# A decoder block on one core: the last LayerNorm split between two phases, new constants in the kernel's clock, and short products traced with a lag

## The chip, the core and the metric

The kernel runs on one NeuronCore of a Trainium2 chip. The metric is the device time of one execution in microseconds (us), the median of several runs. The engines are TensorE (PE: matmuls, with the weight loads as PEld), VectorE (DVE), ScalarE (ACT), GpSimd (POOL) and SyncE (SP), which issues all DMAs. Each engine takes its instructions strictly in the order of its own queue; an instruction waits on semaphores for results of other engines and for DMAs. So the order in each queue, fixed when the program is built, decides who waits for whom.

## The reference

One block with two causal token mixers beside each other, on 2048 tokens of width 1024:

```python
h = _rmsnorm(x, norm_g) * (1 + scale) + shift
p = h @ w_in                       # 9344 columns, split into the parts below
u = val * sigmoid(gate);  u = causal_depthwise_conv(u, width 31)
u = _layernorm(u);  y_conv = (silu(u) * silu(og)) @ w_conv_out
r, k, v, w_low, a_low = token_shift(ts, mu)
o = rwkv7_scan(r, decay, k, v, kk, kk * a)      # 16 heads of 64, a delta-rule state
o = groupnorm(o) + sum(r * k * r_k) * v
y_rwkv = (o * silu(r_og)) @ w_rwkv_out
m = sigmoid(g_conv) * y_conv + sigmoid(g_rwkv) * y_rwkv
x = _rmsnorm(x + gate * (m @ w_out)) * final_g
```

## The kernel before

Tokens are worked on in 4 blocks of 512, features on partitions, 8 tiles of 128 x 512 for 1024 features. Each float32 product is three passes: the weights and the activations are split into a high and a low part (w_hi, w_lo, h_hi, h_lo), and h_hi with w_hi, h_lo with w_hi and h_hi with w_lo are summed, so a projection of one output tile is 8 x 3 = 24 matmuls of 512 columns into a PSUM tile ps_main.

**First phase.** Per block there are 73 projections with w_in. A block has four slots (function `slot`), one for each group of four heads (two pairs). A slot projects k, r and v of both pairs (`proj`, with the token shift in `shifted`), and between them the conv tiles ("c", function `conv`, whose 31 taps are `taps`, VectorE operations on a PSUM tile acc) and the gates ("1" to "4"); `order` and the tables `FILL` and `LAST` set the sequence. The function `pair` makes the operands of the scan out of k, r and v with short products into the PSUM tile aux: lw and la (decay and learning rate), sq (norms of k), KR with BK (two times eight products, masked by VectorE into As), transposes of BK into tk, rh (the bonus term rk) and a transpose of vv. The function `group` then inverts the triangular blocks (POOL's loop over itmp and TT, with detours over DRAM: dA, dT) and runs the chain: 8 chunks, each with a few products into xo, a VectorE addition to uv and four VectorE updates of the state S. After the chain the group norm follows, a transpose (late<-ident,uv), and the result goes to z in DRAM.

Beside these, `side_work` does the next block's RMSNorm, the LayerNorm of the conv branch for the block before (`lnorm_first`: sum of the eight y tiles, mean by a product with ones, squares, variance, rsqrt, then per tile mult, tanh, scale, mult, mult), and splits weights of later products ahead (`presplit`). The LayerNorm of the last block is a task of its own (`last_norm`), which starts when the last convolution is done. Its result u goes to u in DRAM. The phase ends with the output projections of block 0 (`rows0`, "ro" and "co"), which run while the last group's chain ends.

**Order by a clock.** The first phase is not scheduled by the compiler: the program is traced once in Python, and a clock of its own (`note`) counts for every engine when it would be free, with constants for each kind of operation (`RATE`, line 56; a DMA issue counts 0.36 us). `now` is TensorE's time. Every helper is a generator that yields a condition such as `ok(tile)` (ready by the clock); `poll` lets all tasks go on whose condition is met, after each k step (three matmuls) of a projection. A short product outside the chain yields `burst(...)`: it goes at once when its operands are ready, except that during a chain, when no other product has been traced since the last k step, it waits up to `JOIN` = 2.0 us for one:

```python
            if r is None or r > now[0] or joined[0] or not chains[0]:
                return r
            return r + JOIN
```

A slot begins with `until(lambda: not Gs[:-1] or Gs[-2].normed)`: it lets the clock run until the group two before is normalized, whose buffers it takes.

**Second phase.** For each block: the products with w_out into pout (four column parts cb), the residual added into xt, the final RMSNorm and the store of xt; in between the next block's products with w_rwkv_out (`rproj`) and w_conv_out (`cproj`), whose inputs are loaded from z and u in DRAM and split (`lsplit`). Here the order comes from the tile framework's own scheduler. The ring of loads has 8 buffers (`LDB`). The eight xt tiles of a block share their buffers with the eight mr tiles (result of `rproj`) of the next.

In the profile nearly every instruction has line 132, the helper that records it; groups are told apart by their tiles.

Of the kernel before, what the change touches and what calls it, by code (L numbers as in the profile page):

```python
# [45 lines left out]
SLACK = 2.0  # L46
KEPT = ("in",)
# [4 lines left out]
FIRST = 5  # L52
AHEAD = 0.7
BANKS = {"aux": 2, "late": 1, "xo": 2}
SEM, JOIN = 0.1, 2.0
# [19 lines left out]
def hybrid_block(ctx: ExitStack, tc: tile.TileContext, x, vecs, convk, w2a2, final_g, ada, w_in, w_co, w_ro, w_o, crow, out,  # L75
                 seq=2048, groups=(0, 1, 2, 3), phase2=True, dbg=None):
    NB = seq // TB
    now, tasks, kind, joined, chains = [0.0], [], [None], [False], [0]
# [3 lines left out]
    def size(ap):  # L82
        return math.prod(ap.shape[1:])
# [192 lines left out]
    u_dram = scratch("u_d")  # L276

# [245 lines left out]
    hx = Ring(HXB, hx0)  # L523
    t2r = Ring(T2B, lambda name: e2.tile([P, TB], F32, name=name, tag="t2", bufs=T2B))
# [252 lines left out]
    def pair(G, q_, box):  # L777
        b, pr, uv, Asb = G.b, 2 * G.g + q_, G.uv, G.As[q_]
# [37 lines left out]
        yield ok(k)  # L816
        KR = l3.tile([P, NCH // 2, 4 * CH], F32, name="KR", tag="KR", bufs=KRB)
# [75 lines left out]
        yield when(lambda: "v" in box)  # L893
# [14 lines left out]
    def opened(b, g, h, lora):  # L908
        G = Group()
        G.b, G.g, G.h, G.lora, G.tri, G.pairs, G.chained, G.gated, G.normed = b, g, h, lora, 0, 0, False, False, False  # L910
        G.uv = l3.tile([P, NCH, 2, P], F32, name="uv", tag="uv", bufs=2)
        G.dN = dp.tile([2, 2, NCH // 2, 2, 2, 32], F32, name="dN", tag="dN", bufs=3)
        G.As = [l3.tile([P, 2, NCH, P], F32, name="As", tag="As", bufs=ASB) for _ in range(2)]
        G.R = [{}, {}]
        return G
# [4 lines left out]
    def group(G, before):  # L920
        g, b, As, uv, R = G.g, G.b, G.As, G.uv, G.R
# [51 lines left out]
        yield when(lambda: G.pairs == 2 and (before is None or before.chained))  # L973
        yield ok(*As)
# [79 lines left out]
        locked[0] = False  # L1054
# [135 lines left out]
    convs = []  # L1190

    def taps(b, j, u, before):
# [18 lines left out]
    def lnorm_first(b, hx):  # L1211
# [9 lines left out]
        yield hx.room(3, 1)  # L1221
        ys, nxt = yload(0), yload(1)
        for j in range(1, KT):
            yj = nxt
            if j + 1 < KT:
                yield hx.room(1, 1)
                nxt = yload(j + 1)
            yield ok(ys, yj)
            eng.tensor_tensor(out=ys, in0=ys, in1=yj, op=ALU.add)
            hx.give(yj)  # L1230
# [34 lines left out]
        hx.give(qs, rt, mean)  # L1265
        def both_of(j):
            yj, ct = yload(j), hx.take("lnc")
            nc.sync.dma_start(ct, co_dram[b][j])
            return yj, ct

        nxt = None
        for j in range(KT):
            if nxt is None:
                yield hx.room(3, 1)
                nxt = both_of(j)
            else:
                yield hx.room(1)
            yj, ct = nxt
            th, nxt = hx.take("lnth"), None
            if j + 1 < KT and b + 1 == NB and hx.room(2)() is not None:  # L1280
                nxt = both_of(j + 1)
# [80 lines left out]
    def sides(b, g):  # L1362
# [6 lines left out]
        if b and g == (0 if b + 1 == NB else 1):  # L1369
            yield from lnorm_first(b - 1, hx)  # L1370
            if b + 1 == NB:
                yield from lend(3)
# [24 lines left out]
    def last_norm():  # L1397
        yield when(lambda: len(convs) == KT * NB and convs[-1].done)
        yield from lnorm_first(NB - 1, more)
# [14 lines left out]
    def order(b, g):  # L1414
# [11 lines left out]
        for q in range(2):  # L1426
            for name, t_ in (("k", T_K), ("r", T_R), ("vv", T_V)):
                yield name, q, t_ + 2 * g + q
            yield from fill(FIRST if q == 0 else len(todo))
# [16 lines left out]
    def slot(b, g, h, lora, new):  # L1446
        until(lambda: not Gs[:-1] or Gs[-2].normed)
        G = opened(b, g, h, lora)
        reached[0] += 1
        groups_.append(Task(group(G, Gs[-1] if Gs else None), 0))  # L1450
        Gs.append(G)
        items, box, hfs = list(order(b, g)), {}, []
        for n, it in enumerate(items):
            rest = len(items) - n
            if new is not None and rest == 4:
# [121 lines left out]

    def cproj(b, uhl, mhl):
# [41 lines left out]
    for b in range(NB):  # L1620
# [73 lines left out]
        if b + 1 < NB:  # L1694
            uhl = lsplit(u_dram[b + 1], utiles())
# [40 lines left out]
```

## Time and profile before

| | us |
|---|---|
| median of 3 runs (2885.52 to 2889.45) | 2889.28 |
| the profiled execution | 2893.26 |
| its span, first to last instruction | 2891.5 |
| TensorE busy | 2722.4 |
| VectorE busy | 2067.5 |
| GpSimd busy | 1195.6 |
| ScalarE busy | 1092.9 |
| mean granted TensorE clock | 0.984 |

A row of groups reads: line, engine, operation, out<-in tiles, shapes and count, then busy us and mean ns of one, then the engine's idle time just before them and what ended it. A row of waits reads: who waited, for whom, us in total, number of waits, the longest. A row of stretches reads: the stretch and its length, then busy us (and instructions) of PE, PEld, DVE, ACT and POOL, the granted TensorE clock, the DMA share and GB/s.

### The profile page before, as it was taken

The page shows a single profiled execution, that of the slowest core. Times are in us where ns is not written, and L with a number is a line of the kernel's source. Part 1 is how long each engine was busy: PE and PEld are TensorE (multiplying, and loading weights), DVE is VectorE, ACT ScalarE, POOL GpSimd, SP SyncE. Part 2 cuts the span into 40 slices and gives each one's busy share as a digit, 9 for nine tenths or more (in the row PEclk, how much of TensorE's full clock was granted, in tenths as well). Part 3 has the DMA queues.
Part 4 walks back from the last instruction along what each step waited for, and adds up shares of the span by engine and source line. Part 5 has one row for each costly group of instructions (what it writes and reads, how often), then busy time and mean ns, then how long its engine had stood idle before and what let it go on. Part 6 is the DMA issues. An engine that isn't in the chain of part 4 may idle for free. (4 is left out here: it accounts for less than half of the span.)

```text
span 2891.5 us, 52406 instructions
## 1 busy us (share of the span) xinstructions
PE 2722.4 (94%) x19472; PEld 2195.2 (76%) x19472; DVE 2067.5 (72%) x3598; ACT 1092.9 (38%) x2181; POOL 1195.6 (41%) x1725
## 2 busy tenths in 40 slices
PE   6999999989999999999999998999999998999998
PEld 5777777767777777777777776877777777898988
DVE  6877887869677878886878786888887576343343
ACT  5545444434243434443434343324343334121211
POOL 1564746533528364534564553474543612000000
PEclk9999999989999999999999999999999999999999
DMA  8776867666758677767666776676665778777664
GB/s 329 258 286 206 292 218 265 236 233 228 235 185 290 199 255 242 275 222 238 231 251 223 249 255 197 220 269 215 227 230 191 273 247 315 259 239 247 215 226 175
DMA packets 370959, 697.26 MB, mean 241 GB/s; under 512 B 135184, under 2 KB 153936, under 8 KB 370704
## 3 DMA queue, kind: packets, MB, share of 16 engines
q1 hardware_dynamic: 370704, 693.91, 70.3%
q8 instruction: 154, 2.52, 0.4%
q14 instruction: 101, 0.83, 0.1%
HBM read 500.63 MB, written 192.02 MB: 240 GB/s over the span
## 5 line engine op out<-in xcount | busy, mean ns | idle before, releaser
L132 PE MATMUL ps_main<-h_hi,w_hi 128*128 128x512 f32 x2432 | 1016.3, 418 | 16.7 <-DVE lora L132 4.6
L132 PE MATMUL ps_main<-h_hi,w_lo 128*128 128x512 f32 x2432 | 966.9, 398 | 25.3 <-POOL w_lo L132 14.6
L132 PE MATMUL ps_main<-h_lo,w_hi 128*128 128x512 f32 x2432 | 961.3, 395 | 0.5 <-DVE h_lo L132 0.5
L132 DVE SCALAR_TENSOR_TENSOR acc<-u,ck,acc 128x512 f32<-128x512 f32 x928 | 698.0, 752 | 27.9 <-POOL u L132 2.2
L132 PEld LDWEIGHTS ps_main<-h_hi,w_lo 128*128 128x128 f32 x2432 | 462.2, 190 | 140.1 <-POOL w_lo L132 18.7
L132 PEld LDWEIGHTS ps_main<-h_hi,w_hi 128*128 128x128 f32 x2432 | 463.3, 190 | 128.4 <-issue 13.3
L132 PEld LDWEIGHTS ps_main<-h_lo,w_hi 128*128 128x128 f32 x2432 | 463.7, 191 | 96.3 <-issue 8.7
L132 POOL TENSOR_TENSOR w_lo<-w_st,w_hi 128x1024 fp32r<-128x1024 f32 (+1 forms) x82 | 165.0, 2012 | 332.5 <-ACT w_hi L132 288.5
L132 ACT ACTIVATE th<-ps_main 128x512 f32<-128x512 f32 x160 | 95.5, 597 | 360.2 <-PE ps_main L132 311.5
L132 POOL TENSOR_TENSOR TT<-TT,itmp 128x126 f32<-128x126 f32 (+22 forms) x496 | 209.5, 422 | 38.9
L132 POOL TENSOR_TENSOR itmp<-La,TT 128x126 f32<-128x126 f32 (+22 forms) x496 | 203.5, 410 | 37.7 <-issue 7.9
L132 ACT CAST w_hi<-w_st 128x1024 fp32r<-128x1024 f32 (+1 forms) x135 | 127.4, 945 | 221.6 <-DMA w_st<-w_co_t 78.4
L132 DVE SCALAR_TENSOR_TENSOR S<-xo,pe,Se 64x64 f32<-64x64 f32 x512 | 145.0, 283 | 91.9 <-PE xo L132 69.4
L132 ACT COPY uv<-xo 64x256 f32<-64x256 f32 (+1 forms) x192 | 81.2, 439 | 251.3 <-PE xo L132 184.7
L132 DVE TENSOR_TENSOR w_lo<-w_st,w_hi 128x1024 fp32r<-128x1024 f32 x53 | 74.5, 1405 | 68.3 <-PE ps_main L132 51.6
L132 DVE TENSOR_TENSOR As<-aux,maskA 128x512 f32<-128x512 f32 x128 | 82.3, 685 | 49.0 <-PE aux L132 48.9
L132 ACT ACTIVATE Se<-S,pe 128x128 f32<-128x128 f32 x256 | 89.0, 397 | 67.2 <-DVE S L132 66.7
L132 PEld LDWEIGHTS aux<-KR,BK 64*128 64x128 f32 x1024 | 66.3, 191 | 44.3 <-POOL KR L132 21.1
L132 PE MATMUL aux<-KR,BK 64*128 64x128 f32 x1024 | 80.0, 290 | 20.7 <-POOL KR L132 14.0
L132 POOL TENSOR_TENSOR wlo<-wf,wl 64x128 fp32r<-64x128 f32 x64 | 31.3, 489 | 159.2 <-ACT wl L132 156.7
L132 DVE TENSOR_TENSOR xt<-pout,xt 128x256 f32<-128x256 f32 x64 | 24.4, 420 | 100.1 <-PE pout L132 100.1
L132 PEld LDWEIGHTS xo<-S,KR 128*128 128x128 f32 x512 | 77.1, 189 | 20.7 <-ACT Se L132 4.3
(283 smaller groups left out, 5005.4 us busy)
## 6 DMA issues: line engine op xcount, KB each, us to landing
w_hi<-kh_in SPq DMA_DIRECT2D x219, 512.0 KB
w_lo<-kl_in SPq DMA_DIRECT2D x219, 512.0 KB
w_st<-w_in_t SPq DMA_DIRECT2D x73, 512.0 KB
kh_in<-w_hi SPq DMA_DIRECT2D x71, 512.0 KB
kl_in<-w_lo SPq DMA_DIRECT2D x71, 512.0 KB
lny<-y_d SPq DMA_DIRECT2D x96, 256.0 KB
w_hi<-kh_ro SPq DMA_DIRECT2D x32, 512.0 KB
w_lo<-kl_ro SPq DMA_DIRECT2D x32, 512.0 KB
```

The costliest lines, as they stand in the source:

```text
L132: r = f(*a, **k)
```

## The change

Six things are changed.

1. **The lag.** `burst` adds `lag[0]` = `LAG` = 1.0 us to the time at which its operands are ready; with `JOIN` it waits 2.0 as before. From the last slot on the lag is 0.
2. **The clock's constants.** A DMA issue counts 0.45 us instead of 0.36; a ScalarE operation 0.1 us more for each input beyond the first; a scan twice as much per element; a VectorE operation of scalar, tensor and tensor on 64 columns 0.08 us more.
3. **Buffers.** A slot does not wait any more. The pair waits itself: for the chain of the group two before, ahead of As; for its normalization, ahead of uv. La (the inverse's input) waits until the group before has merged its blocks.
4. **The last LayerNorm.** The sum of its y tiles is made as the convolutions end (`taps`, tile ysum). `lnorm_first` of the last block stops after the rsqrt and stores rl in DRAM; what remains is done in the second phase by `ulast`, in place of `lsplit` of u.
5. **Weight splits.** `LATE_W` puts 6, 6 and 4 of them into blocks 1, 2 and 3, where there were 8, 8 and 0; `LEND` lends one buffer to the last LayerNorm instead of three.
6. **The last slot.** After its first pair comes one filling projection instead of five, and the loads of z for `rows0` begin nine items before the slot's end instead of four.

```diff
-            vt["SP"] = t + 0.36
+            vt["SP"] = t + 0.45
...
-            end = vt[name] = t + c0 + c1_ * max([size(out)] + [size(a) for a in ins[:1]])
+            n_ = max([size(out)] + [size(a) for a in ins[:1]])
+            if name == "ACT":
+                c0 += 0.1 * max(len(ins) - 1, 0)
+            elif op == "tensor_tensor_scan":
+                c1_ *= 2
+            elif name == "DVE" and op == "scalar_tensor_tensor" and n_ == CH:
+                c0 += 0.08
+            end = vt[name] = t + c0 + c1_ * n_
...
-            if r is None or r > now[0] or joined[0] or not chains[0]:
+            if r is None:
                 return r
-            return r + JOIN
+            return r + (lag[0] if r + lag[0] > now[0] or joined[0] or not chains[0] else JOIN)
...
+        yield when(lambda: G.prior is None or G.prior.chained)
+        Asb = l3.tile([P, 2, NCH, P], F32, name="As", tag="As", bufs=ASB)
...
-        yield when(lambda: "v" in box)
+        yield when(lambda: "v" in box and (G.prior is None or G.prior.normed))
...
+        yield when(lambda: before is None or before.merged)
         La = lt.tile([P, 32, 32], F32, name="La", tag="La", bufs=1)
...
+        if b + 1 == NB and j == 0:
+            yield hx.room(1)
+            ysum.append(hx.take("ysum"))
+            nc.scalar.copy(ysum[0], yj)
+        elif b + 1 == NB:
+            yield ok(ysum[0], yj)
+            nc.vector.tensor_tensor(out=ysum[0], in0=ysum[0], in1=yj, op=ALU.add)
...
+        if b + 1 == NB:
+            yield ok(rl)
+            nc.sync.dma_start(rl_d, rl)
+            hx.give(rl)
+            return
...
-            for _ in range(0 if b + 1 == NB else (1, 1, 3, 3)[g]):
+            for _ in range(LATE_W[b][g]):
...
-        until(lambda: not Gs[:-1] or Gs[-2].normed)
         G = opened(b, g, h, lora)
         reached[0] += 1
+        if reached[0] == 4 * NB - 1:
+            lag[0] = 0.0
...
+    def ulast(hl):
+        rl = f2.tile([P, TB], F32, name="rl", tag="rl", bufs=1)
+        nc.sync.dma_start(rl, rl_d)
+        for j in range(KT):
+            yt, ct = ldt("yt", y_dram[NB - 1][j]), ldt("ct", co_dram[NB - 1][j])
+            th = ob.tile([P, TB], F32, name="uth", tag="uth")
+            nc.vector.tensor_tensor(out=yt, in0=yt, in1=rl, op=ALU.mult)
+            nc.scalar.activation(th, yt, AF.Tanh, scale=hlg[:, j:j + 1], bias=hlb[:, j:j + 1])
+            nc.scalar.activation(yt, yt, AF.Identity, scale=vc("conv_ln_g", j), bias=vc("conv_ln_b", j))
+            nc.vector.scalar_tensor_tensor(out=yt, in0=th, scalar=1.0, in1=yt, op0=ALU.add, op1=ALU.mult)
+            nc.vector.tensor_tensor(out=yt, in0=yt, in1=ct, op=ALU.mult)
+            split(hl[0][j], hl[1][j], yt, nc.vector)
+        return hl
...
-            uhl = lsplit(u_dram[b + 1], utiles())
+            uhl = lsplit(u_dram[b + 1], utiles()) if b + 2 < NB else ulast(utiles())
```

How the order of instructions moves is seen in three places. The first is TensorE's queue in block 1, second slot, second pair, between the first and the second product of KR with BK (KR and BK are the pair's scan operands; ps_main rows are projection matmuls). Before, from the row after the first product on:

```order
L132 MATMUL ps_main<-h_hi,w_hi 128x512
L132 MATMUL ps_main<-h_lo,w_hi 128x512
L132 MATMUL ps_main<-h_hi,w_lo 128x512
L132 MATMUL ps_main<-h_hi,w_hi 128x512
L132 MATMUL ps_main<-h_lo,w_hi 128x512
L132 MATMUL ps_main<-h_hi,w_lo 128x512
L132 MATMUL aux<-KR,BK 128x128 x8
```

The same place of the changed kernel (xo rows are products of a chain):

```order
L144 MATMUL ps_main<-h_hi,w_hi 128x512
L144 MATMUL ps_main<-h_lo,w_hi 128x512
L144 MATMUL ps_main<-h_hi,w_lo 128x512
L144 MATMUL xo<-uv,tk 64x64 x4
L144 MATMUL xo<-uv,As 64x64 x8
L144 MATMUL ps_main<-h_hi,w_hi 128x512
L144 MATMUL ps_main<-h_lo,w_hi 128x512
L144 MATMUL ps_main<-h_hi,w_lo 128x512
L144 MATMUL ps_main<-h_hi,w_hi 128x512
L144 MATMUL ps_main<-h_lo,w_hi 128x512
L144 MATMUL ps_main<-h_hi,w_lo 128x512
L144 MATMUL aux<-KR,BK 128x128 x8
```

The second product stands behind nine projection matmuls instead of six, and a chain's products have come between.

The second place is SP's queue in the second phase, where block 1 ends (out is the store of xt, kh_ro and kl_ro are halves of split weights of the next block's `rproj`, u_d is u). Before:

```order
L132 DMA w_hi<-kh_ro_11581 128x1024
L132 DMA w_lo<-kl_ro_11582 128x1024
L132 DMA zt<-u_d_4_319 128x512
L132 DMA zt<-u_d_5_320 128x512
L132 DMA zt<-u_d_6_321 128x512
L132 DMA zt<-u_d_7_322 128x512
L132 DMA w_hi<-kh_ro_11785 128x1024
L132 DMA w_lo<-kl_ro_11786 128x1024
L132 DMA out<-xt_26713 128x512
L132 DMA out<-xt_26715 128x512
```

And of the changed kernel (y_d and co_d are the inputs of `ulast`):

```order
L144 DMA ct<-co_d_3_222 128x512
L144 DMA w_hi<-kh_ro_12680 128x1024
L144 DMA w_lo<-kl_ro_12681 128x1024
L144 DMA yt<-y_d_4_191 128x512
L144 DMA ct<-co_d_4_223 128x512
L144 DMA yt<-y_d_5_192 128x512
L144 DMA w_hi<-kh_ro_12860 128x1024
L144 DMA w_lo<-kl_ro_12861 128x1024
L144 DMA ct<-co_d_5_224 128x512
L144 DMA out<-xt_26613 128x512
L144 DMA out<-xt_26615 128x512
```

The stores stand behind the fifth pair of weights (kh_ro_12860) instead of behind the fourth (kh_ro_11785), and behind loads whose buffers VectorE must free.

The third place is VectorE's queue at the same point, just ahead of the scaling of xt by the final RMSNorm (vs, rs and rs_t are its rsqrt). Before:

```order
L132 SCALAR_TENSOR_TENSOR rs_t<-rs_t,vs 128x4
L132 SCALAR_TENSOR_TENSOR rs_27287<-rs_t,rs_27287 128x4
L132 TENSOR_TENSOR rs_t<-rs_27287 128x4
L132 SCALAR_TENSOR_TENSOR rs_t<-rs_t,vs 128x4
L132 SCALAR_TENSOR_TENSOR rs_27287<-rs_t,rs_27287 128x4
L132 SCALAR_TENSOR_TENSOR xt_26713<-xt_26713,rs_27287,fg 128x512
```

And of the changed kernel:

```order
L144 TENSOR_TENSOR rs_t<-rs_27187 128x4
L144 SCALAR_TENSOR_TENSOR yt<-uth,yt 128x512
L144 SCALAR_TENSOR_TENSOR rs_t<-rs_t,vs 128x4
L144 TENSOR_TENSOR yt<-yt,ct 128x512
L144 SCALAR_TENSOR_TENSOR rs_27187<-rs_t,rs_27187 128x4
L144 SCALAR_TENSOR_TENSOR yt<-uth,yt 128x512
L144 TENSOR_TENSOR rs_t<-rs_27187 128x4
L144 TENSOR_TENSOR yt<-yt,ct 128x512
L144 SCALAR_TENSOR_TENSOR rs_t<-rs_t,vs 128x4
L144 TENSOR_TENSOR yt<-yt,rl 128x512
L144 SCALAR_TENSOR_TENSOR rs_27187<-rs_t,rs_27187 128x4
L144 SCALAR_TENSOR_TENSOR xt_26613<-xt_26613,rs_27187,fg 128x512
```

Operations of `ulast` on yt stand between the steps of the rsqrt and ahead of the scaling.

More of the change, by code (lines that the diff above doesn't have):

```diff
@@ L77, in hybrid_block @@
     NB = seq // TB
+    lag = [LAG]
     now, tasks, kind, joined, chains = [0.0], [], [None], [False], [0]
@@ L910, in opened @@
         G.b, G.g, G.h, G.lora, G.tri, G.pairs, G.chained, G.gated, G.normed = b, g, h, lora, 0, 0, False, False, False
-        G.uv = l3.tile([P, NCH, 2, P], F32, name="uv", tag="uv", bufs=2)
+        G.merged = False
+        G.prior, G.uv, G.As = Gs[-2] if len(Gs) > 1 else None, None, []
         G.dN = dp.tile([2, 2, NCH // 2, 2, 2, 32], F32, name="dN", tag="dN", bufs=3)
-        G.As = [l3.tile([P, 2, NCH, P], F32, name="As", tag="As", bufs=ASB) for _ in range(2)]
         G.R = [{}, {}]
@@ L1220, in lnorm_first @@
         eng = nc.vector if b + 1 == NB else nc.gpsimd
[L1221 to L1230, printed above, removed]
+        if ys is None:
+            yield hx.room(3, 1)
+            ys, nxt = yload(0), yload(1)
+            for j in range(1, KT):
+                yj = nxt
+                if j + 1 < KT:
+                    yield hx.room(1, 1)
+                    nxt = yload(j + 1)
+                yield ok(ys, yj)
+                eng.tensor_tensor(out=ys, in0=ys, in1=yj, op=ALU.add)
+                hx.give(yj)
         yield burst(ok(ys), free, bank("late"))
@@ L1264, in lnorm_first @@
                 yield idle("DVE", 0.3)
-        hx.give(qs, rt, mean)
-        def both_of(j):
-            yj, ct = yload(j), hx.take("lnc")
-            nc.sync.dma_start(ct, co_dram[b][j])
[L1269 to L1281, printed above, removed]
+        hx.give(qs, rt)
+        hx1.give(mean)
+        if b + 1 == NB:
[4 more added lines that the diff above has]
+        for j in range(KT):
+            yield hx.room(3, 1)
+            yj, ct, th = yload(j), hx.take("lnc"), hx.take("lnth")
+            nc.sync.dma_start(ct, co_dram[b][j])
             yield ok(yj, rl)
@@ L1371, in sides @@
             if b + 1 == NB:
-                yield from lend(3)
+                yield from lend(LEND)
         if b:
-            for _ in range(0 if b + 1 == NB else (1, 1, 3, 3)[g]):
+            for _ in range(LATE_W[b][g]):
                 n_ = later.pop(0)
@@ L1398, in last_norm @@
         yield when(lambda: len(convs) == KT * NB and convs[-1].done)
-        yield from lnorm_first(NB - 1, more)
+        yield from lnorm_first(NB - 1, more, ysum[0])
     def proj(h, ti, name, box):
@@ L1428, in order @@
                 yield name, q, t_ + 2 * g + q
-            yield from fill(FIRST if q == 0 else len(todo))
+            yield from fill(len(todo) if q else FIRST_LAST if (b, g) == (NB - 1, 3) else FIRST)
     T_OF = {"1": T_ROG, "2": T_COG, "3": T_GR, "4": T_GC}
@@ L1454, in slot @@
             rest = len(items) - n
-            if new is not None and rest == 4:
+            if new is not None and rest == (4 if b + 1 < NB else HLAST):
                 if b + 1 < NB:
@@ L1576, in lsplit @@
         return hi, lo
+    def ulast(hl):
+        rl = f2.tile([P, TB], F32, name="rl", tag="rl", bufs=1)
+        nc.sync.dma_start(rl, rl_d)
+        for j in range(KT):
+            yt, ct = ldt("yt", y_dram[NB - 1][j]), ldt("ct", co_dram[NB - 1][j])
[7 more added lines that the diff above has]
+        return hl
     def cproj(b, uhl, mhl):
```

23 lines of the change are left out of this document (17 added, 6 removed).

## The prediction

> **What bounds the kernel now.** I read the page first (busy shares), then four stretches of the program, then what TensorE waited for, then the clock it was granted around its longest waits.
>
> ```profile
> span 2891.5 us, 52406 instructions
> PE 2722.4 (94%) x19472; PEld 2195.2 (76%) x19472; DVE 2067.5 (72%) x3598; ACT 1092.9 (38%) x2181; POOL 1195.6 (41%) x1725
> ```
> ```profile
> 0.00:600.00 600.00, 541.41 (x3669) 426.16 (x3670) 469.99 (x790) 278.47 (x511) 317.50 (x407) 0.97 0.75 263
> 600.00:2300.00 1700.00, 1623.85 (x12256) 1282.82 (x12255) 1320.05 (x2305) 667.87 (x1365) 841.38 (x1286) 0.99 0.69 233
> 2300.00:2420.00 120.00, 110.11 (x863) 87.24 (x861) 91.16 (x147) 43.26 (x73) 36.72 (x34) 0.99 0.74 250
> 2420.00:2892.00 472.00, 447.08 (x2689) 398.97 (x2688) 186.28 (x358) 103.33 (x232) 0.00 (x0) 0.98 0.69 239
> ```
>
> TensorE (first number after the stretch's length) is busy 2722.4 of 2891.5 us; the other engines are far below. It has the same 19472 products after the change, so the time can only come from the 169.1 us in which it idles and from the clock. The idle time is 58.6 us in the first block, 76.2 in the next 1700 us, 9.9 in the first phase's tail and 24.9 in the second phase (the last line's length less its busy time). Who ended it:
>
> ```profile
> PE ps_main L132 <- POOL w_lo L132: 14.6, 8, 4.6
> PE aux L132 <- POOL KR L132: 14.0, 14, 2.0
> PE aux L132 <- ACT sq L132: 12.9, 13, 3.2
> PE late L132 <- DVE Tn L132: 12.1, 8, 3.3
> PE aux L132 <- DVE As L132: 6.3, 8, 2.7
> PE xo L132 <- DVE uv L132: 6.1, 9, 2.0
> PE ps_main L132 <- DVE w_lo L132: 5.0, 4, 1.9
> PE ps_main L132 <- ACT w_hi L132: 4.3, 2, 2.7
> PE late L132 <- POOL uv L132: 4.2, 5, 1.6
> PE aux L132 <- ACT tk L132: 4.0, 10, 1.5
> PE aux L132 <- POOL wlo L132: 3.5, 6, 1.3
> PE aux L132 <- ACT wl L132: 3.0, 2, 2.7
> PE ps_main L132 <- ACT h_hi L132: 2.8, 1, 2.8
> PE xo L132 <- DVE S L132: 2.1, 3, 1.2
> PE late L132 <- POOL lny L132: 1.6, 2, 1.2
> PE late L132 <- ACT xTs L132: 0.6, 2, 0.3
> PE late L132 <- POOL lnq L132: 0.4, 1, 0.4
> ```
>
> Total us, number of waits, longest. Tiles aux and late are the short products outside the chain (late<-Tn is the chain's). Leaving Tn out, the aux and late rows sum to 14.0 + 12.9 + 6.3 + 4.2 + 4.0 + 3.5 + 3.0 + 1.6 + 0.6 + 0.4 = 50.5 us. These are many waits of about 1 us: the product stood in TensorE's queue just before its operand was there.
>
> **The sum, part by part.** Durations are of the profiled execution: 2893.26 us, 4.0 above the median of 2889.28. I work out a difference and take it from both.
>
> *The lag.* Every burst (a short product that is not in the chain) is now traced 1.0 us after the kernel's clock has its operands ready, up to the last slot. What that covers is bounded by the rows: at most the whole 50.5, less what the longest waits keep beyond 1.0 us (KR 1.0, sq 2.2, As 1.7, uv 0.6, tk 0.5, wlo 0.3, wl 1.7, lny 0.2: 8.2), so 42.3; at least nothing, if the operands come later by as much. The orders show which is nearer: against the projection matmuls most of these products stand 6 to 50 matmuls later, while the projections that produce k, r and v stand where they did; a matmul starts every 0.23 us:
>
> ```profile
> 2390.03 0.39 PE L132 MATMUL ps_main<-h_lo,w_hi 128*128 128x512 f32 x1
> 2390.26 0.39 PE L132 MATMUL ps_main<-h_hi,w_lo 128*128 128x512 f32 x1
> ...
> 2404.19 0.48 PE L132 MATMUL ps_main<-h_hi,w_hi 128*128 128x512 f32 x1
> ```
>
> The second KR product of a pair follows the first after 12 matmuls in most pairs, before after 6: 1.4 us more for the mask products on VectorE that must free its bank. But operands that come out of an earlier short product (tk, rk, ssr) are now later too. I take three quarters of the bound: **-32 us**.
>
> *The clock it takes along.* Four of those waits are followed by a lower granted clock:
>
> ```profile
> 194.00:204.00 10.00, 7.34 (x34) 5.80 (x34) 8.10 (x14) 1.63 (x2) 6.03 (x6) 0.67 0.94 337
> 1041.00:1051.00 10.00, 6.77 (x16) 4.33 (x16) 8.27 (x11) 5.66 (x10) 7.03 (x13) 0.66 0.39 146
> 1191.00:1201.00 10.00, 7.27 (x19) 5.27 (x19) 5.24 (x9) 5.34 (x10) 2.24 (x5) 0.66 0.81 269
> 1484.00:1490.00 6.00, 3.98 (x25) 2.83 (x26) 5.14 (x6) 0.62 (x1) 5.84 (x8) 0.80 0.37 126
> ```
>
> The third number from the end is the clock: 10 x 0.33 + 10 x 0.34 + 10 x 0.34 + 6 x 0.20 = 11.3 us of clock lost, behind waits of 2.7 (As), 3.2 (sq), 2.7 (wl) and 2.0 us (KR). Less 1.0 us each, only sq's stays over 2; three of four go: **-8 us**, ends 0 and -11.3. The Trainium skill ("TensorE: Matmul & The Clock Gate", Part 1) says that the clock falls to half after at least one idle window of about 3.4 us. By that rule none of these four waits is long enough, this term would be 0, and the whole 8 us more; the four rows with 0.66 to 0.80 disagree, so I keep the term.
>
> *The newly fitted constants.* The scan, the two-operand activation and the 64-column S update were set too short by the kernel's clock:
>
> ```profile
> L132 DVE TENSOR_TENSOR_SCAN M<-keep,M 128x512 f32<-128x512 f32 x32 | 44.4, 1388 | 8.4 <-ACT M L132 8.1
> L132 ACT ACTIVATE t<-ps_main,mu 128x512 f32<-128x512 f32 x96 | 65.9, 686 | 58.8 <-PE ps_main L132 52.7 <-issue 5.5
> L132 DVE SCALAR_TENSOR_TENSOR S<-xo,pe,Se 64x64 f32<-64x64 f32 x512 | 145.0, 283 | 91.9 <-PE xo L132 69.4 <-ACT Se L132 5.7 <-issue 1.8
> L132 DVE SCALAR_TENSOR_TENSOR acc<-u,ck,acc 128x512 f32<-128x512 f32 x928 | 698.0, 752 | 27.9 <-POOL u L132 2.2
> ```
>
> By line 56 the scan counts 0.15 + 512 x 0.0011 = 0.71 us where the row has 1.388; now 1.28. The activation goes from 0.56 to 0.66 (row 0.686), S from 0.22 to 0.30 (row 0.283). The orders spread the 16 chains over 117 more matmuls in all, 7 each. What that can save is the chain's own waits, DVE uv 6.1 and S 2.1, 8.2 us: I take **-5**, ends 0 and -8.2. A DMA issue counts 0.45 instead of 0.36; ahead of Tn stand eight As loads, so 0.7 us on each of 8 waits of 12.1 us in all: **-4**, ends 0 and -12.1.
>
> *Tail of the first phase.* The last projections' weights see five of the eight z loads earlier in SP's queue; the 2.8 us for h_hi ends at the fifth: **-2**, since the other three stand where they did. The last LayerNorm's second half (mult, STT, mult for 8 tiles) leaves VectorE there. TensorE idles 9.9 us in that stretch, 2.8 of it counted; I take **-2** (the one long wait for VectorE's uv, 2.0), ends 0 and -7. SP and POOL get four weight splits there instead, with TensorE's weights among them; their cover is the slack of 36.7 busy us on POOL in 120.
>
> *Weights of the first block.* POOL w_lo, DVE w_lo and ACT w_hi wait 23.9 us. Nothing in the change aims at them, but the order moves them: splits that stand inside POOL's inverse loop go from 5 to 7. Ends: -24 and, at up to 4.6 us for each of two more, +9. I take **0**, the middle being close to it.
>
> *Edits that I cost at nothing.* The slot's wait for the group two before is gone, and the pair waits for its buffers instead. The old wait stood in the order at one slot's start, and what it cost there is in the row POOL uv; the pairs' new waits stop no projection as long as the last chain ends in time, and by the order it still ends 66 projection matmuls (15 us) before the phase does, instead of 81. The sum for the last LayerNorm's mean is added tap row by tap row (7 adds on VectorE and one ScalarE copy in place of 7 adds and 8 loads): the same adds, earlier. Four of sixteen weight splits go from blocks 1 and 2 to block 3, where POOL did less; the cover is that POOL is busy 841 of 1700 us, and without it each half split would hold the next POOL operand by about as much as a w_lo wait above, 1 to 2 us. The last slot's earlier second pair moves 48 matmuls of projections only.
>
> *Second phase.* The second half of the LayerNorm is done here: 8 y and 8 co loads instead of 8 u loads, and 24 VectorE and 16 ScalarE operations more. By the order it lands at the end of block 1, where the time is already tight:
>
> ```profile
> 2616.66 5.39 DVE L132 SCALAR_TENSOR_TENSOR xt<-xt,rs,fg 128x512 f32<-128x512 f32 x8
> 2617.53 0.38 SPq L132 DMA_DIRECT2D w_lo<-kl_ro  x1
> 2618.01 4.98 SPq L132 DMA_DIRECT2D out<-xt  x6
> ...
> 2624.66 0.69 DVE L132 SCALAR_TENSOR_TENSOR mr<-rth,ps_main 128x512 f32<-128x512 f32 x1 [2.61 <-DMA out<-xt]
> ...
> 2625.41 0.50 PE L132 MATMUL ps_main<-o_hi,w_hi 128*128 128x512 f32 x1 [2.49 <-DVE mr L132]
> ```
>
> mr takes over the buffer of xt, so it waits for the first out store, 6.6 us after its issue; TensorE idles 2.49 us for mr, from 2622.9. Now 12 of the new operations stand ahead of xt's scaling on VectorE (12 x 5.39 / 8 = 8.1 us, starting at 2624.8), and on SP the stores stand behind the fifth weight pair, which waits until TensorE has done its second row, at 2622.9. Store issued at about 2625.5 instead of 2618.0, landing 5 to 6.6 us later, mr, TensorE at about 2631.5: 8.5 us of idling instead of 2.5, and at that length a lower clock as in the rows above, 2 to 3 us. **+8**, ends 0 (the loads land early and VectorE's operations fit between) and +17. The final u split is where it was. Twelve more passages from projection to short product (490 instead of 478): the matmul after one lasts 0.48 instead of 0.39, so 0.2 us for both sides: **+2**.
>
> Sum: -32 - 8 - 5 - 4 - 2 - 2 + 8 + 2 = **-43 us**: 2850 for an execution like the profiled one, **2846** against the median.
>
> **The rivals.**
>
> *The lag covers nothing.* If the queues of POOL and ACT, not the constants, make operands late, each product waits as before at its new place; the 32 and 8 go and the sum is -3: 2886. For it: KR's waits are ended by POOL, whose constants are unchanged. Against: the mean wait is 1.0 us and k, r, v did not move.
>
> *It covers all.* 42 + 11 + 8 + 12 + 4, half of the weights' 24, less 10: -79, 2810. For it: long waits and clock drops go together. Against: in a new order new misses appear.
>
> *Slower: chains fall between taps.* Short products and chains are 20 to 40 us later by the order, so each chain's 128 steps meet other convolution taps, 0.752 us each (acc's row). One more tap ahead of a step delays the next TensorE step by that. It cancels the gain from 43 / 0.752 = 57 steps on; with 90 of 128, +68 - 43 = +25: 2914. For it: VectorE is busy 1320 of 1700 us. Against: now such waits are 8.2 us over all steps, and the S constant is longer.
>
> **How the numbers follow.** Forecast (2830 to 2868): 0.58. Covers all: 0.16. Covers nothing: 0.14. Slower: 0.12. About 0.2%, 5.8 us, is what a measurement of this kernel can tell from no change. Faster 0.58 + 0.16 = 0.74, same 0.14, slower 0.12. The range reaches from the second case to just past the third: 2810 to 2888; the forecast's own bounds lie within it.
>
> **What would show it.** In the profile after: the aux and late rows without Tn at 14 to 22 us in all, KR and sq shortest; 0.66 gone around the pairs' products; xo's waits at 3 to 4; one TensorE wait of 6 us or more for mr at the end of block 1 in the second phase. Wrong would be: aux rows over 35, xo's waits over 30, or weights' rows changed by over 15 either way.

## The result, and the profile after

The changed kernel takes 2849.39 us (median of 4 runs, 2847.64 to 2858.5), the kernel before beside it 2887.60 us (2885.52 to 2889.45). The ratio is 0.987, 95% interval 0.9848 to 0.9892: 38 us less, where 43 were forecast (2846). The profiled executions, from which all rows and stages below come, differ by more: 2893.26 - 2847.64 = 45.6 us.

The page after begins (span; busy time, share and count of each engine):

```profile
span 2845.9 us, 52351 instructions
PE 2696.9 (95%) x19472; PEld 2198.8 (77%) x19472; DVE 2046.1 (72%) x3596; ACT 1087.4 (38%) x2182; POOL 1196.2 (42%) x1727
```

The same 19472 products are busy for 25.5 us less than before (2722.4), and TensorE idles 149.0 us instead of 169.1. More than half of the gain of the profiled pair stands in a number that I had taken as fixed. By shape, two groups before (busy us, mean ns, then idle time ahead):

```profile
L132 PE MATMUL aux<-sq,bones 128*128 128x512 f32 x64 | 35.8, 642 | 13.0 <-ACT sq L132 12.9
L132 PE MATMUL aux<-rh,bones 128*128 128x512 f32 x32 | 16.1, 504 | 5.0 <-ACT tk L132 3.4
```

and after:

```profile
L144 PE MATMUL aux<-sq,bones 128*128 128x512 f32 x64 | 33.2, 600 | 1.6 <-ACT sq L144 1.6
L144 PE MATMUL aux<-rh,bones 128*128 128x512 f32 x32 | 13.5, 421 | 0.6 <-ACT tk L144 0.5
```

The records of these products are themselves shorter in the run where they wait less. And records overlap: a projection matmul's lasts 0.39 us while the next starts after 0.23, so the first 0.16 us of a wait behind one lie inside a busy record. The Trainium skill ("Perfetto Trace Analysis", Identifying the Most-Contended Engine) says that the busy share of matmuls is not a good measure of how close a kernel is to its roofline, since matmuls are pipelined. In this pair of pages the busy time moved by 25.5 us with the work unchanged. So I also measured from the start of one product to the start of the next, over the whole trace. By this measure the short products outside the chain (without those of its opening) gained 57.7 us, the chain's (xo) 11.6, and the chain's opening products lost 16.5.

The stretches after, with TensorE's busy time first and the clock third from the end (the first phase now ends at 2363):

```profile
0.00:600.00 600.00, 543.06 (x3711) 433.94 (x3712) 457.91 (x783) 278.43 (x519) 314.20 (x396) 0.97 0.76 265
600.00:2300.00 1700.00, 1640.75 (x12735) 1312.76 (x12734) 1343.83 (x2358) 669.40 (x1373) 848.20 (x1313) 0.99 0.72 238
2300.00:2363.00 63.00, 60.98 (x342) 48.92 (x342) 43.63 (x76) 25.04 (x45) 33.80 (x18) 1.00 0.57 185
2363.00:2846.00 483.00, 452.15 (x2687) 403.16 (x2687) 200.76 (x382) 114.54 (x246) 0.00 (x0) 0.97 0.70 239
```

In the same 1700 us TensorE does 12735 products instead of 12256. What ended its waits (total, number, longest; rows without bearing on the argument are left out):

```profile
PE late L144 <- DVE Tn L144: 22.7, 9, 5.1
PE ps_main L144 <- POOL w_lo L144: 15.4, 6, 5.0
PE ps_main L144 <- DVE mr L144: 13.0, 3, 9.3
PE aux L144 <- POOL KR L144: 8.0, 7, 1.9
PE ps_main L144 <- ACT w_hi L144: 7.8, 3, 5.5
PE xo L144 <- DVE uv L144: 5.0, 7, 1.4
PE aux L144 <- POOL wlo L144: 3.8, 4, 1.9
PE late L144 <- POOL uv L144: 3.4, 3, 1.8
PE ps_main L144 <- DVE w_lo L144: 3.1, 5, 1.2
PE late L144 <- POOL lny L144: 2.0, 1, 2.0
PE aux L144 <- ACT sq L144: 1.6, 3, 0.9
PE xo L144 <- DVE S L144: 1.3, 2, 0.9
PE aux L144 <- DVE As L144: 0.8, 1, 0.8
PE aux L144 <- ACT tk L144: 0.5, 1, 0.5
```

The aux and late rows without Tn sum to 20.1 us instead of 50.5 (both sums leave out the "issue" rows, 5.0 and 2.4 us, in which the profile shows nothing that was waited for). Tn has grown from 12.1 to 22.7, mr from 5.5 to 13.0. The granted clock around the longest of these waits, and around two waits of 1.9 us for KR (first and fifth row):

```profile
760.00:770.00 10.00, 8.15 (x51) 6.09 (x50) 7.64 (x11) 0.62 (x1) 6.67 (x12) 0.83 0.61 63
790.00:800.00 10.00, 7.11 (x101) 5.81 (x103) 7.50 (x15) 0.24 (x1) 0.00 (x0) 0.66 0.79 268
1335.00:1345.00 10.00, 9.45 (x152) 7.68 (x153) 7.17 (x22) 0.00 (x0) 0.00 (x0) 0.83 0.67 230
1476.00:1486.00 10.00, 10.00 (x172) 7.98 (x176) 6.78 (x12) 1.39 (x3) 3.57 (x3) 0.83 1.02 352
1868.00:1878.00 10.00, 10.00 (x63) 8.03 (x64) 8.94 (x14) 0.52 (x2) 9.50 (x17) 0.83 0.83 309
2043.00:2053.00 10.00, 7.86 (x135) 6.50 (x137) 5.61 (x11) 3.11 (x6) 2.60 (x4) 0.66 0.78 277
2572.00:2583.00 11.00, 5.64 (x14) 4.44 (x15) 8.49 (x14) 1.66 (x3) 0.00 (x0) 0.53 0.93 329
```

The drops have moved with the waits: to Tn (790, 1335, 1476, 2043) and mr (2572). Two of 0.83 stand behind KR (760, 1868). The stall for mr at the end of block 1 in the timeline of the changed kernel (start, duration, instruction; in brackets the idle time before it):

```profile
2570.11 5.39 DVE L144 SCALAR_TENSOR_TENSOR xt<-xt,rs,fg 128x512 f32<-128x512 f32 x8
2570.89 5.46 SPq L144 DMA_DIRECT2D out<-xt  x8
2576.63 1.28 DVE L144 SCALAR_TENSOR_TENSOR mr<-rth,ps_main 128x512 f32<-128x512 f32 x2
...
2577.36 0.79 PE L144 MATMUL ps_main<-o_hi,w_hi 128*128 128x512 f32 x1 [9.33 <-DVE mr L144]
```

The first store goes out at 2570.9, mr is written 5.7 us later, and TensorE idles 9.3 us; the granted clock over these 11 us is 0.53.

### The profile page after: what moved, and what is told of

Read it like the earlier page. It is cut to its first block, busy times and chain, and to the rows that moved or that the text cites. A ratio compares the mean times of both kernels' runs of the same rounds, so it can differ in the third digit from the quotient of the medians.

```text
span 2845.9 us, 52351 instructions
## 1 busy us (share of the span) xinstructions
PE 2696.9 (95%) x19472; PEld 2198.8 (77%) x19472; DVE 2046.1 (72%) x3596; ACT 1087.4 (38%) x2182; POOL 1196.2 (42%) x1727
## 5 line engine op out<-in xcount | busy, mean ns | idle before, releaser
L144 PE MATMUL ps_main<-h_hi,w_lo 128*128 128x512 f32 x2432 | 966.2, 397 | 20.1 <-POOL w_lo L144 15.4
L144 ACT ACTIVATE t<-ps_main,mu 128x512 f32<-128x512 f32 x96 | 65.7, 685 | 80.8 <-PE ps_main L144 60.9
L144 PEld LDWEIGHTS xo<-uv,tk 128*64 128x64 f32 (+1 forms) x768 | 55.9, 154 | 43.5 <-DVE uv L144 24.5
L144 PEld LDWEIGHTS aux<-KR,BK 64*128 64x128 f32 x1024 | 63.8, 189 | 29.4 <-POOL KR L144 13.4
```

Of the source, the lines that this page charges most:

```text
L144: r = f(*a, **k)
```

## The experiments

Each kernel ran in five rounds against the kernel before. The stage times come from the profiled executions: the start of the 400th projection matmul from the end of the first phase ("to -400"), from there to the first pout product ("tail"), and from each block's first pout product to the next one's ("block 0", "block 1"); what follows is 189 to 190 us everywhere. "Bursts" is the sum of TensorE's waits for aux and late without Tn. Differences of time between two runs are taken from their ratios below, since the kernel before took 2887.60 to 2892.23 us beside the different runs.

```
                         ratio   interval          to -400  tail   block 0 block 1  bursts  Tn    mr
before                   1                          2296.3  124.5   144.7   136.5    50.5  12.1   5.5
changed                  0.987   0.9848 to 0.9892   2245.1  117.5   148.0   145.8    20.1  22.7  13.0
e1  lag 0                0.9907  0.9889 to 0.9924   2255.3  123.0   145.6   145.1    34.8   4.3  12.1
e2  lag alone            0.9958  0.9944 to 0.9973   2266.9  127.0   150.8   140.6    39.8  14.2   7.4
e3  old constants        0.9949  0.9934 to 0.9964   2270.3  125.2   147.0   147.1    36.1  16.7  13.1
e4  second half back     0.99    0.9883 to 0.9918   2248.4  147.3   141.0   136.9    21.4  22.5   7.1
e5  lag 1.1              0.9927  0.9907 to 0.9946   2252.9  138.6   142.4   145.1    29.4  13.8  13.0
e6  Tn lag               0.9829  0.9809 to 0.9849   2227.8  124.1   151.6   146.7    21.6   3.1  13.9
e7  rl held back         0.9836  0.9815 to 0.9858   2251.9  119.8   150.1   139.9    20.6  23.3   7.5
e8  DMA issue 0.36       0.9901  0.9884 to 0.9918   2257.4  121.4   147.1   145.2    25.7  17.9  13.1
e9  old LayerNorm        0.9889  0.987 to 0.9907    2234.8  157.1   140.2   139.1    25.2  13.3   7.7
e10 Tn lag and rl        0.9791  0.9771 to 0.9811   2227.0  122.7   153.1   140.3    20.4   3.0   8.6
e11 lag and constants    1.0018  1.0 to 1.0036      2271.5  129.1   154.6   137.0    43.0  15.4  11.5
e12 lag 0 and Tn lag     0.9924  0.99 to 0.9947     2259.6  118.3   145.4   146.6    36.9   0.9  13.1
```

How far one execution can be trusted: e7 has the changed kernel's order throughout the first phase, and its profiled execution is 6.8 us later at -400 (and is the slowest of its five, 2852.93 against a median of 2844.18; e11's is the fastest of twelve, 2883.53 against 2894.92).

**e1: the lag undone**

```diff
-SEM, JOIN, LAG = 0.1, 2.0, 1.0
+SEM, JOIN, LAG = 0.1, 2.0, 0.0
```

> The changed kernel (2849) with the lag at 0 and all else kept. Theory (the lag carries the gain: -32 of waits and -8 of clock in the prediction): the waits of TensorE for aux and late operands without Tn go from 20 us back to about 50, and the time to 2880-2892. Rival (the other edits moved the order and that alone removed the misses): these waits stay under 30 us and the time within 2845-2860.

2862.60 us lies between the theory and the rival: undoing the lag costs 0.0037 of the time here, 11 us, not 40, and the two intervals just overlap. Of the 30.4 us by which the burst waits fell, 15.7 fall without it. The waits of this kernel:

```profile
PE aux L144 <- POOL KR L144: 22.1, 12, 7.1
PE aux L144 <- ACT tk L144: 5.0, 8, 1.5
PE late L144 <- DVE Tn L144: 4.3, 6, 2.5
PE aux L144 <- ACT sq L144: 3.1, 6, 0.8
```

sq, 12.9 before, is mostly gone without any lag (3.1). KR is what the lag shortens between these two orders (22.1 to 8.0), and Tn grows by more than that (4.3 to 22.7).

**e2: the lag alone, on the kernel before**

```diff
-            if r is None or r > now[0] or joined[0] or not chains[0]:
+            if r is None:
                 return r
-            return r + JOIN
+            return r + (lag[0] if r + lag[0] > now[0] or joined[0] or not chains[0] else JOIN)
```

> The kernel before (2888) with the lag of 1.0 us alone, 0 from the last slot on; old constants, old buffers, old last LayerNorm. Theory: the lag carries the gain, so 2840-2856, aux and late waits without Tn 15-25 us. Rival (the lag needs the other edits, the pairs' own buffer waits above all, since the old slot wait stands in its way): 2870-2888.

2878.52 us: 12 us of gain. Again neither the whole nor nothing; the rival's range holds it. KR and sq shrink here too (7.8 and 2.5), so sq falls with the lag alone as well as with the other edits alone (e1).

**e3 and e8: the old constants; and SP's alone**

```diff
-            vt["SP"] = t + 0.45
+            vt["SP"] = t + 0.36
...
-            if name == "ACT":
-                c0 += 0.1 * max(len(ins) - 1, 0)
-            elif op == "tensor_tensor_scan":
-                c1_ *= 2
-            elif name == "DVE" and op == "scalar_tensor_tensor" and n_ == CH:
-                c0 += 0.08
```

> The changed kernel with the old constants of the clock (DMA issue 0.36, no extra for ScalarE inputs, scan and 64-column update). By the prediction's terms (chain -5, Tn -4) it should lose 9 us: 2858, Tn's waits more than 22.7 us, xo's waits for uv and S back to 8. Rival (the constants do nothing, Tn's waits come from elsewhere): 2844-2854 with Tn's waits anywhere between 10 and 23.

> The changed kernel with a DMA issue counted 0.36 us again, the other three constants new. Old constants in all four places cost 27 us. Theory (the engine constants place the bursts, SP's constant only Tn and some loads): 2850-2857, 0.987-0.989 of before, aux and late waits without Tn under 26 us. Rival (it is SP's constant): 0.992-0.996, and these waits at 35 or more.

2877.88 us with all old, 2862.95 with SP's alone (the first line of the diff). Undoing them costs 0.79 and 0.31% of the time, 23 and 9 us, against 9 expected for all. Neither run bears out its theory or its rival in full: e3's time is beyond both, and e8's time lies between them, with the bursts (25.7) as the theory had them. The gain is not in the waits that I named: Tn is shorter with the old constants (16.7), uv and S wait 1.9 us more in all (8.2 against 6.3). It is in the bursts (36.1 against 20.1 us).

**e4 and e9: the last LayerNorm back in the first phase**

e4 moves only its second half back; e9 undoes the whole edit (the old sum and the old loads, not shown in the diff) with its buffers and the split weights per slot.

```diff
-        if b + 1 == NB:
-            yield ok(rl)
-            nc.sync.dma_start(rl_d, rl)
-            hx.give(rl)
-            return
...
-            uhl = lsplit(u_dram[b + 1], utiles()) if b + 2 < NB else ulast(utiles())
+            uhl = lsplit(u_dram[b + 1], utiles())
```

and, in e9 alone:

```diff
-LEND = 1
-LATE_W = ((), (1, 1, 2, 2), (1, 1, 2, 2), (1, 1, 1, 1))
+LEND = 3
+LATE_W = ((), (1, 1, 3, 3), (1, 1, 3, 3), (0, 0, 0, 0))
```

> The changed kernel with the second half of the last LayerNorm back in the first phase (mult, tanh, scale, mult, mult and the store of u there; the second phase loads u). By the prediction (second phase +8, tail of the first -2): 6 us faster, 2843, with TensorE's wait for mr back from 13.0 to 5-6 us. Rival (VectorE's 24 operations cost the first phase's tail as much or more): 2849-2860, mr's waits short, but xo or pout waits in the tail longer by 5 or more.

> The changed kernel with the old last LayerNorm in full (loads and sum in the first phase, three lent buffers, u in DRAM, old split weights per slot). In the run with only its second half moved back and one lent buffer, the last 400 projections up to pout took 147 us (changed kernel 117, before 124) and the second phase 457 (473, 460). Theory (what cost there was the one buffer, not the LayerNorm's operations): tail 120-128 us, second phase 455-462, so 5-8 us faster than the changed kernel, 0.983-0.987. Rival (the first phase can't hide the operations since its chains come later now): tail over 135 and 0.989 or more.

2863.40 and 2859.20 us: by the ratios 9 and 5 us slower than the changed kernel, though the intervals overlap. So neither brought the gain of my theory, and the tail tells why, as the rivals had it. Block 1 of the second phase gets back 7 to 9 us as I had it, and block 0 another 7 to 8, but the tail grows from 117.5 to 147 and 157 us. TensorE's only wait in e9 between 2360 and 2395 us:

```profile
PE pout L144 <- ACT o_hi L144: 26.4, 1, 26.4
```

and the timeline of its ScalarE up to there:

```profile
2385.86 0.81 ACT L144 ACTIVATE lnth<-lny,hlb,hlg 128x512 f32<-128x512 f32 x1 [2.09 <-DVE lny L144]
2386.70 0.81 ACT L144 ACTIVATE lny<-lny,v 128x512 f32<-128x512 f32 x1
2389.60 0.81 ACT L144 ACTIVATE lnth<-lny,hlb,hlg 128x512 f32<-128x512 f32 x1 [2.09 <-DVE lny L144]
2390.50 0.81 ACT L144 ACTIVATE lny<-lny,v 128x512 f32<-128x512 f32 x1
2391.22 3.20 ACT L144 CAST o_hi<-mr 128x512 fp32r<-128x512 f32 x6
```

o_hi, the operand of the first pout product, stands in ScalarE's queue behind all eight tiles of the LayerNorm, 3.7 us each at the end. In the kernel before, the last tanh (lnth) and the first pout product stand here:

```profile
2409.48 0.82 ACT L132 ACTIVATE lnth<-lny,hlb,hlg 128x512 f32<-128x512 f32 x1 [2.64 <-DVE lny L132]
2420.80 0.38 PE L132 MATMUL pout<-w_hi,o_hi 128*128 128x256 f32 x1 [0.71 <-ACT o_hi L132]
```

That is 10 us to spare. The first phase has since lost some 50 us up to -400, the LayerNorm (196 us from the last tap to the last tanh before, 250 in e9) has not.

**e5: a lag of 1.1**

```diff
-SEM, JOIN, LAG = 0.1, 2.0, 1.0
+SEM, JOIN, LAG = 0.1, 2.0, 1.1
```

> The changed kernel with a lag of 1.1 us in place of 1.0: a change without a purpose, to see what a slightly different order is worth by itself. Theory (undoing one part, which cost 9 to 27 us in the runs so far, measured that part): within 4 us of the changed kernel, 0.986-0.989 of before, Tn's waits near 22 and aux and late waits without Tn near 21. Rival (each new order draws new misses, so the differences of single parts are mostly luck): 8 us or more away on either side, with Tn's or the weights' waits changed by 5 or more.

2871.39 us: 16 us slower than with 1.0, the rival's case. The new order draws 10.0 us more at KR, one wait of 6.3 among them, and 8.8 us for o_hi in the tail. So a change without a purpose moves this kernel by more than the undoing of most single parts (0.0057 of the time, against 0.0019 to 0.0037 in e1, e4, e8 and e9; only e3's 0.0079 is more), and the single figures of these runs can't be read as the worth of the part. The waits move too: the bursts by 9.3 us, Tn by 8.9.

**e6 and e12: the chain's opening later**

```diff
-                yield both(ok(Tn, uv), free, bank("late"), bank("aux", 2), bank("xo", 2))
+                yield later_by(TNLAG, both(ok(Tn, uv), free, bank("late"), bank("aux", 2), bank("xo", 2)))
```

`later_by` adds TNLAG = 2.0 us up to the last slot; e12 has LAG = 0 as well.

> The changed kernel with 2.0 us added to the time at which the clock has the chain's first products (late<-Tn,As) ready, up to the last slot. Theory (the clock has the reload of As over DRAM too early, and with the lag on the bursts nothing else holds the chain back any more): Tn's waits from 22.7 to under 8 us, the time 10-15 us less, 0.982-0.984 of before. Rival (VectorE's transposes come as much later as the product, or the chain's later start is paid at the next group): Tn's waits stay over 15 or others grow by as much, time within 5 us of the changed kernel.

> The changed kernel with the lag at 0 and 2.0 us more for the chain's first products. Theory (the lag saves 31 us start to start at the bursts and gives 24 back at the chain's first products, which wait only 4 us for Tn when the lag is 0; so their own lag can gain only with the bursts' lag): 0.989-0.992 like lag 0 alone, aux and late waits without Tn 30-40 us. Rival (the 2.0 us are worth 10 us in any order, or the order's luck decides): 0.983-0.987.

e6: 2841.51 us, Tn's waits 3.1 instead of 22.7, and -400 is reached 17.3 us earlier; e10 repeats both (3.0 us, 18.1). The theory holds for the first phase, though KR grows to 14.0 us and the tail by 6.6. e12: 2867.68 us, no better than e1. In these orders there is little to gain at Tn with the lag at 0 (4.3 us in e1): the second lag paid only together with the first. Why the bursts' lag lengthens the waits for Tn was not settled.

**e7: ulast kept off the end of block 1**

```diff
+            if b + 3 == NB:
+                rl_t = f2.tile([P, TB], F32, name="rl", tag="rl", bufs=1)
+                nc.vector.tensor_copy(rl_t[:, 0:NTT], rall)
```

`ulast` then loads rl into this tile, so the load waits for the copy.

> The changed kernel with the load of rl held back until block 1 of the second phase has its rsqrt (a copy of four columns into rl's buffer ahead of the load), so that no operation of ulast stands ahead of the scaling of xt or of the out stores. Theory (the prediction's term for the second phase): the wait for mr at the end of block 1 from 9.3 us to 2-4, mr's waits in all from 13.0 to 5-8, the time 6-10 us less. Rival (the stores wait for the weights' pair on SP or for DMA bandwidth and not for VectorE): mr's longest wait stays over 7 us, time unchanged.

2844.18 us, 10 us less by the ratio. mr's waits are 7.5 us (longest 4.0); the one at the end of block 1 is 3.2 us instead of 9.3 (2.5 in the kernel before). Block 1 takes 139.9 us instead of 145.8, and in e10 140.3. About 6 us of the stall were ulast's operations and loads. The two gains, of e6 and e7, are of the size that an order alone can move (e5); what speaks for them is that the row and the stage that were named moved as forecast, and that both come again in e10.

**e10: both together**

> The changed kernel with both 2.0 us more for the chain's first products and rl's load behind the rsqrt of block 1. Theory (one stands in the first phase, the other in the second, so they add): Tn's waits under 8, mr's waits 5-9 in all, 0.979-0.982 of before, 2830-2840. Rival (the chain of waits passes on what is saved): 0.983 or more, like either alone.

2829.88 us (2827.13 to 2834.51), 0.9791 of before and clearly below the changed kernel's interval: the fastest of all, by about the sum of e6 and e7. Some of its waits:

```profile
PE aux L144 <- POOL KR L144: 12.6, 8, 2.9
PE ps_main L144 <- DVE th L144: 10.6, 4, 3.9
PE ps_main L144 <- DVE mr L144: 8.6, 3, 4.2
PE pout L144 <- DMA w_hi<-kh_o: 7.2, 1, 7.2
```

Neither Tn nor mr leads any more; a load of w_out's weights at the change of phases is new against the changed kernel (e6 has it too, 5.9 us).

**e11: the lag and the constants, nothing else**

The edits of e2 and the reverse of e3's diff, on the kernel before. So edits 3 to 6 of the change are all missing.

> The kernel before with the lag and all four new constants, but with the old slot wait, old last LayerNorm, old splits and old last slot. Theory (the prediction's terms lag, clock and constants, -49, and no cost in the second phase): 0.984-0.988. Rival (lag alone gave 0.9958 since the slots' wait for the group two before takes the later pairs' time away again; the buffers have to change with it): 0.992-0.997.

No gain: 1.0018, outside the theory's range and beyond the rival's. The rival named a cause, the slots' wait for the group two before. While the program is traced, the kernel's clock shows by how much it jumps at that wait, with no projection traced meanwhile (us, sum over 16 slots):

```
before                 3.4   (slot 2,0: 3.37)
lag alone             15.7   (0,2: 1.46; 2,0: 3.51; 2,3: 10.69)
lag and constants     33.9   (1,0: 3.17; 2,0: 8.53; 3,0: 7.32; 3,2: 13.38; 3,3: 1.46)
```

On the chip, TensorE's timeline in e11 at slot 3,2 (block and slot counted from 0; the clock says 2006):

```profile
1980.95 0.39 PE L140 MATMUL ps_main<-h_hi,w_lo 128*128 128x512 f32 x1
1981.17 0.60 PE L140 MATMUL late<-ident,uv 128*128 128x128 f32 x4
1990.79 2.08 PE L140 MATMUL late<-lnq,ones 128*128 128x512 f32 x2 [9.02 <-POOL lnq L140]
1996.25 1.12 PE L140 MATMUL late<-ident,uv 128*128 128x128 f32 x4 [3.38 <-DVE lnq L140]
1997.02 0.78 PE L140 MATMUL ps_main<-h_hi,w_hi 128*128 128x512 f32 x1
```

For 16 us ten short products and no projection: what the clock had jumped over, 13.4 us, TensorE really waits, 12.4. In e2 there is a wait at 1591 us, where its slot 2,3 begins (the clock says 1580 and jumps 10.7):

```profile
PE aux L133 <- ACT wl L133: 6.3, 1, 6.3
```

and in the kernel before one at 1195 us, slot 2,0 (clock 1167, jump 3.4):

```profile
PE aux L132 <- ACT wl L132: 2.7, 1, 2.7
```

The slots' wait is not all. The profiled execution of e11, its fastest, is still 25 us ahead of the kernel before at -400 (26 behind the changed kernel) and gives 15 of them back in the tail and in block 0, much of it in one wait:

```profile
PE pout L140 <- DVE xt L140: 14.0, 1, 14.0
```

The loads of xt go out only at 2412.9, behind a store of z at 2411.1 in SP's queue. No run has edit 3, 5 or 6 alone, so how much of e11's loss each of them would mend is open.

## Why the prediction was right, and where it wasn't

The sum holds by stage in the profiled pair. Up to -400 the terms lag, clock, constants and passages gave -32 - 8 - 9 + 2 = -47 us; measured 2245.1 - 2296.3 = -51.2. The tail: -4, measured -7.0. The second phase: +8, measured +12.6, of which block 1 is 9.3 and block 0 is 3.3. By cause it holds less:

- **Lag, -32.** The rows fell by 30.4 us, and 20.1 us remain where 14 to 22 were named. But that is not all the lag's: undoing it brings 14.7 us back (e1), and alone it takes 10.7 (e2). The step that failed is "against the projection matmuls most of these products stand 6 to 50 matmuls later, while the projections that produce k, r and v stand where they did", from which I took three quarters of the bound: it gave the rows' fall to the lag alone, when undoing the constants brings 16.0 us back as well (e3). Nor was the bound of 42.3 us one: it was made of idle time, and start to start these products gained 57.7 us, the clock included. KR did not become the shortest row but stayed the longest of them.
- **Clock, -8.** Wrong in sign. The clock lost is (1 - 0.984) x 2891.5 = 46 us before and (1 - 0.981) x 2845.9 = 54 after, some of it while TensorE idled. The waits behind the named drops did get shorter, but "Less 1.0 us each, only sq's stays over 2" failed as a reason: after waits of 1.9 us for KR the clock is still 0.83 over 10 us (760, 1868), and longer waits for Tn and mr brought new drops. By the Trainium skill's rule ("TensorE: Matmul & The Clock Gate", Part 1: at least one idle window of about 3.4 us) the term would have been 0, closer to the truth. The rule is not the reason, though: the drop at 1335 follows a wait of 2.1 us.
- **Constants.** The chain's own waits fell by 1.9 us (8.2 to 6.3) for the 5 expected; Tn's rose by 10.6 where 4 less were expected. Where the lag is off, Tn's waits are shorter (12.1 before, 4.3 in e1), but no run has the constant of the DMA issue alone there, and with the lag on, setting it back shortens them too (17.9 in e8). So the term for Tn is not borne out.
- **Weights of the first block, 0.** The three rows went from 23.9 to 15.4 + 3.1 + 7.8 = 26.3 us: +2.4.
- **Second phase, +8.** Mechanism right, and the size for block 1: one wait of 9.3 us for mr at its end (8.5 forecast), behind stores and operations of ulast, and e7 takes all but 3.2 of it away. The 3.3 us of block 0 were not in the prediction; its granted clock is 0.95 there instead of 0.98, and no run was made of it.
- **Edits costed at nothing, and the LayerNorm's -2.** Here the working failed most, without touching the sum. I priced the slots' wait and the LayerNorm's second half in the order of before, where they cost about 3 and 2 us. In the order that the other edits make they weigh more. Without edits 3 to 6 the lag and the constants gain nothing, and the slots' wait is seen in that run (e11). With the old LayerNorm the tail is 30 to 40 us longer, of which blocks 0 and 1 give 14 to 16 back (e4, e9). In all, moving it gained 5 to 9 us where the working had it cost 6, though that difference is within what another order can bring (e5). I had also put the slots' wait in the wrong row (POOL uv; it is wl, 2.7 us).
- **The rivals.** The chains did not fall between VectorE's taps: uv and S wait 6.3 us in all. Covering nothing (2886) and covering all (2810) lie 37 and 39 us away.

That the sum met is partly cancelling: start to start the short products gained 57.7 us where 32 stood and the chain's 11.6 where 5 stood, while Tn, the clock and the second phase gave back more than forecast. It is also partly luck: the lag of 1.1 (e5) shows that an order no better reasoned lands 16 us away, and the median came within 4 us of the forecast.

## What to carry to other kernels

Price an edit that removes a wait or moves work in the order that the rest of the change makes, not in the old one: what has 10 us to spare before can be the bound once the rest is 50 us faster. Undo the parts one at a time and also try a change without a purpose, since in a kernel ordered by a clock a tenth of a microsecond can be worth as much as a part. After a gain, read the wait rows again: the rows that grew (Tn, mr) named the two small edits that gave another 20 us.

## What the runs showed of the hardware

The busy time of TensorE is no constant of its work: 19472 products took 2722.4 us of records before and 2696.9 after, at a slightly lower mean clock. The first 0.16 us of a wait behind a projection matmul (0.39 us of record, 0.23 from start to start) do not appear as idle time, so rows of idle time understate what short products cost; starts counted against starts do not. The granted clock was 0.83 over 10 us after idle times of 1.9, 2.1 and 2.4 us (at 760, 1335 and 1476 in the changed kernel), and 0.53 over 11 us that hold more than half of an idle time of 9.3 (at 2572).
